# Gates of two branches as tile pairs with seven half-size products, in a phase of their own; branch sums kept in SBUF

## The chip, the core and the metric

The kernel runs on one core of one Trainium2 chip. A core has a matrix engine (PE), a vector engine (DVE), a scalar engine (ACT), a general engine (POOL) and an engine that mainly issues transfers (SP). Each runs its own list of instructions in order and waits for the others by semaphores. The time is device microseconds from start to end of one execution; a kernel's time is the median over its runs.

## What is computed

One decoder layer over 1024 tokens of width 1024, in float32:

```python
h    = rms_norm(x, g1)
proj = h @ w_in                        # heads of all branches, and 3 x 1024 gate logits
y_a  = rwkv7_branch(...)               # state recurrence over the tokens
y_b  = stick_breaking_branch(...)      # 8 heads of 64
y_m  = memory_branch(...)              # 4 heads of 128 on 256 memory tokens
branch_out = einsum('btnc,ncd->btnd', [y_a, y_b, y_m], w_branch)
merged = sum_b sigmoid(gate_logits_b) * branch_out_b
x = x + merged @ w_out
x = x + conv_ffn(rms_norm(x, g2), ...) # up-projection, causal convolution, SwiGLU, down-projection
```

The change touches the gate logits (`h @ w_in[:, gates]`), the sigmoid behind them, and the sum over the branches.

## The kernel before

The whole program is written out as one list per engine, with no loop left on the chip. Activations stand transposed in SBUF: 8 tiles of 128 channels x 1024 tokens, each split into a high part `xhi` and a low rest `xlo` that PE reads at its full speed. A weight tile of 128 output columns (`wr`, 128x1024) is split in the same way into `wh` and `wl`: ACT makes the high part (L83), POOL or DVE the rest (L89, L86). A float32 product is then three matmuls: hi by hi, lo by hi, hi by lo. The tokens' norm `rbc` is multiplied in behind the product.

A **gate** tile (`gate_item`, one branch b and one group d of 128 outputs) is such a projection: 8 channel tiles x 2 token halves x 3 = 48 matmuls of 128x512 into two PSUM banks "mm". ACT copies both banks to SBUF (L885), DVE multiplies with `rbc` (L886), ACT takes the sigmoid (L889), and for most gates the result goes to DRAM (`gsd`). There are 3 x 8 gates, 1152 such matmuls.

The order of the program is made by **weaving**: `weave(main, filler, ratio)` lets the main generator write one step and then as many steps of the filler as the ratio says. A filler step is one channel tile of a projection (6 matmuls) or of a branch (6 matmuls). The filler `pump` runs through a list `items`: projections of the rwkv branch, V, K and Q of stick-breaking, gates, the memory branch's projections, and the branch products (`branch_item`: y times `w_br`, 24 matmuls). The stages on the main side are `rwkv_prep` (four times), `sb_attn` (stick-breaking, L961), `mem_attn` (L1191), `stage2` (the state recurrence: 16 chunks of three steps, L601), `group_norm`. Behind them stand `branch_last`, `out_proj`, `up_phase` and `down_phase` with no weave.

Two places matter below. In `sb_qk` the K projection's two PSUM banks are copied by ACT and squared (`k_fin`), and then `k_ss` sums the squares over the heads with 32 small matmuls (`g<-kon,w` 64x2) on PE; in `items` a gate stands between the two (`kp, gate, kss`). And behind the memory branch `items` has three gates (`gate(sp1), gate(), gate()`) ahead of branch 1, whose input y was written to DRAM (`yd`) and is loaded again (`A<-yd`, `load_y`), split by ACT and DVE.

The sums over the branches go through a DRAM tensor `mrd`: branch 1 writes, branch 2 reads, adds and writes, `branch_last` reads.

PSUM has eight banks: four named "mm" for projections, four named "g" for everything else.

## Time and profile before

| | |
|---|---|
| time, median of 3 runs | 1786.67 us (1786.48 to 1787.19) |
| profiled execution: first to last instruction | 1785.0 us |
| PE busy | 1775.7 us, 99% |
| DVE / ACT / POOL busy | 1184.1 / 882.8 / 697.1 us |
| granted clock of PE, mean | 1.000 |
| `rwkv_prep` and before it | 0 to about 317 us |
| `sb_attn` | about 318 to 612 us |
| `mem_attn` | about 612 to 749 us |
| gates, first branch products | 749 to 785 us |
| `stage2` | about 785 to 983 us |
| the rest, to the end | 983 to 1785 us |

A row of the groups reads: line, engine, operation, output tile <- input tiles, shapes, count | busy us, mean ns of one | idle time of the engine just ahead of them and what ended it. The duration of a matmul in these rows is longer than its pitch, because matmuls overlap; its cost in a dense stretch is the stretch over the count. Line numbers with "of before" below are those of the kernel before; the changed kernel has other numbers.

### The profile page before, as it was taken

What the parts mean: (1) busy time and instruction counts of PE and PEld (TensorE: products, weight loads), DVE (VectorE), ACT (ScalarE), POOL (GpSimd) and SP (SyncE); (2) the same over time, 40 slices, a digit from 0 to 9 for tenths busy, and PEclk for the clock granted to TensorE, in tenths of its full rate; (3) what the DMA queues carried; (4) which work ended last, traced back from release to release, by engine and by line L of the source; (5) the groups of instructions that cost most, each with busy time, mean ns of one, the idle gap of its engine ahead of it and who ended that gap; (6) DMA issues with size and microseconds to landing.
All of it is one profiled execution on the core that took longest, in us unless ns stands there. A gap on an engine that the chain in (4) does not pass through costs nothing.

```text
span 1785.0 us, 27451 instructions
## 1 busy us (share of the span) xinstructions
PE 1775.7 (99%) x10481; PEld 1442.9 (81%) x10481; DVE 1184.1 (66%) x1687; ACT 882.8 (49%) x1667; POOL 697.1 (39%) x409
## 2 busy tenths in 40 slices
PE   9999999999999999999999999999999999999999
PEld 7777778878888888787777888888888888888887
DVE  5666674787888655243533882697767777795596
ACT  6543344466566635444556434454444445444343
POOL 1232252322221012022333322257777677545454
PEclk9999999999999999999999999999999999999999
DMA  4256574111112343658764662323323333396475
GB/s 185 72 167 188 180 247 152 51 56 43 54 57 69 111 126 93 201 181 280 264 229 146 236 210 98 115 89 124 101 89 110 109 109 113 109 330 219 142 248 200
DMA packets 120758, 263.39 MB, mean 148 GB/s; under 512 B 28330, under 2 KB 41130, under 8 KB 120499
## 3 DMA queue, kind: packets, MB, share of 16 engines
q1 hardware_dynamic: 82434, 193.31, 32.9%
q10 hardware_dynamic: 34416, 55.72, 8.5%
q0 software_dynamic: 3776, 12.62, 2.4%
q8 instruction: 82, 1.34, 0.3%
q14 instruction: 50, 0.40, 0.1%
HBM read 180.04 MB, written 81.53 MB: 147 GB/s over the span
## 4 chain that ended last, share of the span: by engine, by line
PE 62%; issue 1%; POOL 1%; ACT 1%; DVE 1%; DMA 0%; ACTq 0%; DVEq 0%; POOLq 0%; SPq 0%
PE mm L139 53%; PE g L139 8%; PE g L122 1%; POOL dw L1856 1%; DVE qk L715 0%; ACT wh L83 0%; DMA qk<-vd 0%; ACT w L885 0%; DVE w L886 0%; DVE keep L1876 0%; POOL l L1555 0%; ACT qk L664 0%; ACT ys L1020 0%; DVE wl L86 0%; ACT qk L1059 0%
## 5 line engine op out<-in xcount | busy, mean ns | idle before, releaser
L89 POOL TENSOR_TENSOR wl<-wr,wh 128x1024 fp32r<-128x1024 f32 x58 | 148.0, 2552 | 368.2 <-ACT wh L83 360.5
L139 PE MATMUL mm<-xhi,wh 128*128 128x512 f32 x784 | 260.6, 413 | 0.5 <-ACT w L936 0.4
L139 PE MATMUL mm<-xlo,wh 128*128 128x512 f32 x784 | 243.5, 392 | 0.7 <-DVE xlo L225 0.6
L139 PE MATMUL mm<-xhi,wl 128*128 128x512 f32 x784 | 242.2, 390 | 0.0
L139 PEld LDWEIGHTS mm<-xlo,wh 128*128 128x128 f32 x784 | 147.0, 188 | 34.0 <-DVE xlo L225 1.6
L139 PEld LDWEIGHTS mm<-xhi,wl 128*128 128x128 f32 x784 | 147.1, 188 | 32.6
L139 PEld LDWEIGHTS mm<-xhi,wh 128*128 128x128 f32 x784 | 136.5, 189 | 30.4 <-issue 7.9
L139 PE MATMUL mm<-dw,da 128*128 128x512 f32 x528 | 121.1, 390 | 0.0
L83 ACT ACTIVATE wh<-wr 128x1024 fp32r<-128x1024 f32 x75 | 79.5, 1060 | 81.0 <-PE mm L139 61.9
L139 PE MATMUL mm<-BT,l 128*128 128x512 f32 x504 | 118.0, 389 | 0.3 <-POOL l L1555 0.3
L139 PEld LDWEIGHTS mm<-dw,da 128*128 128x128 f32 x528 | 98.9, 188 | 21.7 <-DVE da L1855 1.2
L1856 POOL TENSOR_TENSOR dw<-draw,dw 128x512 fp32r<-128x512 f32 x55 | 83.1, 1520 | 77.0 <-ACT dw L1854 74.2
L985 DVE TENSOR_TENSOR_SCAN at<-at,at 128x128 f32<-128x128 f32 (+3 forms) x64 | 91.0, 1429 | 33.1 <-ACT at L979 33.0
L139 PEld LDWEIGHTS mm<-BT,l 128*128 128x128 f32 x504 | 94.5, 188 | 20.3 <-POOL l L1555 0.7
L139 PE MATMUL mm<-BT,wh 128*128 128x512 f32 x352 | 108.5, 389 | 0.1
L139 PE MATMUL mm<-B,wh 128*128 128x512 f32 x352 | 108.4, 389 | 0.0
L195 POOL TENSOR_TENSOR hf<-rs,half 128x16 f32<-128x16 f32 (+1 forms) x18 | 49.2, 2732 | 143.4 <-DVE rs L192 138.9
L1855 DVE TENSOR_TENSOR da<-draw,da 128x512 fp32r<-128x512 f32 x77 | 66.6, 873 | 49.0 <-ACT da L1853 48.6
L139 PE MATMUL g<-dw,da 128*128 128x512 f32 x396 | 90.5, 389 | 0.4 <-POOL dw L1856 0.4
L1853 ACT ACTIVATE da<-draw 128x512 fp32r<-128x512 f32 x77 | 48.3, 628 | 81.0 <-PE mm L139 31.7
L139 PEld LDWEIGHTS g<-dw,da 128*128 128x128 f32 x396 | 74.2, 188 | 16.2 <-POOL dw L1856 0.8
L1627 ACT ACTIVATE g<-u,params 128x512 f32<-128x512 f32 x88 | 65.2, 770 | 32.1 <-DVE u L1717 22.9
(345 smaller groups left out, 3956.6 us busy)
## 6 DMA issues: line engine op xcount, KB each, us to landing
wr<-in_w_in_dram SPq DMA_DIRECT2D x49, 512.0 KB, 3.8
draw<-actd SPq DMA_DIRECT2D x77, 256.0 KB, 3.1
at<-scr SPq DMA_DIRECT2D x28, 512.0 KB, 5.5
draw<-in_w_down_dram SPq DMA_DIRECT2D x55, 256.0 KB, 4.6
rw<-in_w_up_dram SPq DMA_DIRECT2D x22, 512.0 KB, 3.5
actd<-gall ACTq DMA_DIRECT2D x41, 256.0 KB, 3.1
gsd<-w ACTq DMA_DIRECT2D x20, 512.0 KB, 2.8
wr<-in_w_up_dram SPq DMA_DIRECT2D x18, 512.0 KB, 3.6
```

The source lines that it names most:

```text
L83: ins = self.nc.scalar.activation(hi, raw, AF.Copy)
L89: self.last_wl = self.nc.gpsimd.tensor_tensor(lo, raw, hi.bitcast(F32), ALU.subtract)
L122: self.pinned(self.nc.tensor.transpose(out, in_, self.ident[:n, :n]))
L139: self.pinned(self.nc.tensor.matmul(*a, **k))
L195: nc.gpsimd.tensor_tensor(out, t[:, :n], self.half[:, :n], ALU.pow)
L985: self.pinned(nc.vector.tensor_tensor_scan(sn[:, :W][:, ::-1], sn[:, :W][:, ::-1], self.smask[:, 1024 - W :][:, ::-1], 1.0, ALU.mult, ALU. ...
L1627: keep(nc.scalar.activation(c, u[:, 2 + h * 512 : 514 + h * 512], AF.Identity, scale=self.par("cw2", m), bias=self.par("cb", m)))
L1853: self.pinned(nc.scalar.activation(A[:, 0], a, AF.Copy))
L1855: self.pinned(nc.vector.tensor_tensor(A[:, 1], a, A[:, 0].bitcast(F32), ALU.subtract))
L1856: nc.gpsimd.tensor_tensor(Wt[:, 1], w, Wt[:, 0].bitcast(F32), ALU.subtract)
```

## The change

**Gate pairs.** The 16 gates of branches 1 and 2 are computed in pairs (d, d+1) with seven products of half size in place of eight: each is 4 channel tiles x 3 matmuls of 128x512, so 84 matmuls stand for 96. The left sides are `w1`, `w2` and sums of their halves, made per pair by POOL and split by ACT and POOL (`prep1` to `prep3`); the right sides are the halves of h and sums of these (`T12`, `T34`), made once by `x_sums` from the input that is loaded again. Products 1 and 2, 6 and 7, 5 and 3 share a PSUM bank; ACT and DVE add up the results, and all gates go to `gsd`.

**The phase.** `x_sums` is woven with V and three gates of branch 0 (`early`); `gate_pairs` follows, between `rwkv_prep` and `sb_attn`, with steps of the inversion (`inv`, DVE) beside it. The gates between K's projection and `kss` are gone, as are two of the three behind the memory branch. The weaves have new ratios: 0.55 for 1.03 (`sb_attn`), 1.4 for 1.6 (`mem_attn`), 1.1 for 2.08 (`stage2`).

**Sums in SBUF.** `mrd` is gone: the sums stay in tiles of `pool_l`, which is opened ahead of `stage2`, when h is no longer needed. The transfers of `inst<-mad` and `td<-inst` move from POOL's queue to SP's, and V is loaded again for its differences instead of being kept.

On PE the change takes 96 matmuls of 128x512 away and adds none.

```diff
@@ -896,7 +899,172 @@
...
+    def x_sums(self, gp):
+        nc = self.nc
+        self.T12, self.T34 = [], []
+        tags = iter(["qk"] * 8 + ["at"] * 7 + ["A"])
...
+        load(0)
+        for p in range(4):
+            nc.sync.dma_start(self.inst[p * 32 : p * 32 + 32], self.mad[p * 32 : p * 32 + 32])
+        yield
+        for k in range(4):
+            if k < 3:
+                load(k + 1)
+            x, z = raws.pop(k)
+            for t, i in ((x, k), (z, k + 4)):
+                self.pinned(nc.scalar.activation(t, t, AF.Copy, scale=self.par("g1", i)))
+            if k > 1:
+                next(gp)
+            yield
+            t12, t34 = self.t4(), self.t4()
+            sub(t12[:, L], x[:, R], x[:, L])
+            sub(t12[:, R], z[:, R], t12[:, L])
+            sub(t34[:, L], z[:, R], x[:, R])
+            sub(t34[:, R], t12[:, R], z[:, L])
+            yield
+            for t, out, eng in ((t12, self.T12, nc.vector), (t34, self.T34, nc.gpsimd)):
+                hi, lo = self.t4(next(tags), F32R), self.t4(next(tags), F32R)
+                self.pinned(nc.scalar.activation(hi, t, AF.Copy))
+                self.pinned(eng.tensor_tensor(lo, t, hi.bitcast(F32), ALU.subtract))
+                out.append((hi, lo))
+            yield
+        next(gp)
...
+    def gate_pairs(self, pairs, inv, steps, after):
...
+        X = (self.xhi, self.xlo)
+        plain = lambda k0, c: lambda v, k: X[v][k0 + k][:, c]
+        made = lambda T, c: lambda v, k: T[k][v][:, c]
+        side = {1: plain(0, L), 2: plain(4, L), 3: plain(4, R), 4: made(self.T34, R), 5: made(self.T12, L), 6: made(self.T12, R), 7: made(self.T34, L)}
+        pt = lambda o, x, y, op: nc.gpsimd.tensor_tensor(o, x, y, op)
+        vt = lambda o, x, y, op=ALU.add: self.pinned(nc.vector.tensor_tensor(o, x, y, op))
+
...
+        def prep1(n):
+            w = split(W[n][0], wt("wh"), wt("wl"))
+            st[n, 1], st[n, 2] = [[x[:, c] for x in w] for c in (L, R)]
+
+        def prep2(n):
+            w1, w2 = W[n]
+            s = st[n, "s"] = self.t4()
+            pt(s[:, L], w2[:, L], w2[:, R], ALU.add)
+            pt(s[:, R], s[:, L], w1[:, L], ALU.subtract)
+            w = split(s, self.t4("A", F32R), self.t4("A", F32R))
+            st[n, 5], st[n, 6] = [[x[:, c] for x in w] for c in (L, R)]
+
+        def prep3(n):
+            w1, w2 = W.pop(n)
+            s = st.pop((n, "s"))
+            pt(w2[:, L], w1[:, L], w2[:, L], ALU.subtract)
+            pt(w1[:, R], w1[:, R], s[:, R], ALU.subtract)
+            w = split(w2, wt("wh"), wt("wl"))
+            st[n, 7], st[n, 4] = [[x[:, c] for x in w] for c in (L, R)]
+            s4 = self.t4("A", F32R)
+            st[n, 3] = split(w1[:, R], s4[:, L], s4[:, R])
+
+        def product(n, i, bank, first):
+            w = st.pop((n, i))
+            for k in range(4):
+                for pi, (u, v) in enumerate(((0, 0), (0, 1), (1, 0))):
+                    self.mmul(bank, w[u][:, k * 128 : (k + 1) * 128], side[i](v, k), start=(first and k == 0 and pi == 0),
+                              stop=(k == 3 and pi == 2), skip_group_check=not first)
+
+        def finish(n, i, g):
+            b, d = pairs[n]
+            self.pinned(nc.scalar.activation(g, g, AF.Sigmoid))
+            nc.scalar.dma_start(self.gsd[b, d + i], g)
+
+        def step(n, i):
+            if i == 1:
+                A = st[n, "A"] = self.ps("mm")
+                product(n, 1, A, True)
+                st[n, "p1"] = self.t4("ys", n=512)
+                self.pinned(nc.scalar.activation(st[n, "p1"], A, AF.Copy))
...
+                B = st[n, "B"] = self.ps("mm")
+                product(n, 6, B, True)
+                u = st[n, "u"] = self.t4()
+                vt(u[:, R], B, st[n, "p1"])
...
+            elif i == 7:
+                B = st.pop((n, "B"))
+                product(n, 7, B, False)
+                v = st[n, "v"] = self.t4()
+                vt(v[:, L], B, st.pop((n, "p1")))
+                vt(v[:, R], st[n, "C"], v[:, L])
...
+            else:
+                C = st.pop((n, "C"))
+                product(n, 3, C, False)
+                u = st.pop((n, "u"))
+                vt(u[:, R], C, u[:, R])
+                vt(u[:, R], u[:, R], self.rbc[:, R], ALU.mult)
+                finish(n, 0, u)
...
+        for f in (load, prep1, prep2, prep3):
+            f(0)
+            if f != prep3:
+                yield
+        load(1)
+        due = 0.0
+        for n in range(len(pairs)):
+            for i in (1, 5, 6, 2, 7, 4, 3):
+                step(n, i)
+                if n + 1 == len(pairs):
+                    if i == 7:
+                        next(after)
+                else:
+                    if i == 2:
+                        prep1(n + 1)
+                    elif i == 7:
+                        prep2(n + 1)
+                    elif i == 3:
+                        prep3(n + 1)
+                        load(n + 2)
+                due += steps
+                while due >= 1.0:
+                    due -= 1.0
+                    next(inv, None)
+                yield
@@ -954,9 +1122,8 @@
 
         w = self.I["w_in"]
         hooks = {1: lambda: k_split(1), 3: q_ss, 4: lambda: q_split(0), 6: lambda: q_split(1)}
-        kq = {4: k_bc, 5: lambda: k_split(0)} if p else {5: k_bc, 6: lambda: k_split(0)}
-        kh = {} if p else {k: functools.partial(self.difference, k - 3) for k in (3, 4, 5, 6)}
-        return self.proj_item(w[18 + p], k_fin, kh), k_ss, self.proj_item(w[14 + p], q_fin, kq), hooks
+        kq = {4: k_bc, 5: lambda: k_split(0)} if p else {5: k_bc, 6: lambda: k_split(0)} | {k: functools.partial(self.difference, k - 1) for k in (1, 2, 3, 4)}
+        return self.proj_item(w[18 + p], k_fin, before), k_ss, self.proj_item(w[14 + p], q_fin, kq), hooks
@@ -1274,40 +1441,36 @@
...
+            yield
+        if first:
+            self.merged.append(self.part("o") if d < 5 else g)
+        out = self.merged[d] if first else g
         for h in range(2):
             hs = slice(h * 512, (h + 1) * 512)
-            self.pinned(nc.vector.tensor_tensor(g[:, hs], pp[h], g[:, hs], ALU.mult))
+            self.pinned(nc.vector.tensor_tensor(out[:, hs], pp[h], g[:, hs], ALU.mult))
         if not first:
-            (nc.vector if d == 7 else nc.gpsimd).tensor_tensor(g, g, o, ALU.add)
-        nc.gpsimd.dma_start(self.mrd[d], g)
@@ -1970,49 +2138,49 @@
...
-        gq = [(b, d) for b in (1, 0) for d in range(8)]
-        gq[14:14] = [(2, d) for d in range(4)]
-        self.stored = set(gq)
...
+        gq = [(0, d) for d in range(8)]
...
+        items = [self.shift_item(i + p, krv[p], f"{n}{p}") for p in range(4) for n, i in (("k", 4), ("r", 0), ("v", 8)) if (p, n) != (0, "k")]
+        items += [*self.sb_v(), gate(), gate(), gate()]
+        early = self.stream(items)
+        items = []
+        hooks = {0: self.differ}
         for p in range(4):
-            kp, kss, qp, hooks = self.sb_qk(p, qk[p])
-            items += [*([self.differ] if p == 0 else []), kp, gate({4: self.spread_last} if p == 0 else {}), kss, qp, gate(hooks), mark(f"sb{p}")]
+            kp, kss, qp, after = self.sb_qk(p, qk[p], hooks)
+            items += [kp, *([mark(f"sb{p - 1}")] if p else []), kss, qp]
+            hooks = after | ({5: self.spread_last} if p == 0 else {})
         prep, mss, mv, mk = self.mem_kv()
...
-            mqi[h] = self.mem_q(h, mq[h], {2: mqi[h - 1][1], 4: mark(f"mq{h - 1}")} if h > 1 else {})
-        items += [gate({0: prep[0], 5: prep[1]}), gate(), lambda: setattr(self, "low_dve", True), gate({2: prep[0], 6: prep[1]}), mss, *mv, *mk, mqi[0][0], mark("kv")]
-        items += [self.mem_kss, gate({3: mqi[0][1]}), self.mem_kbc, mqi[1][0], mark("mq0")]
-        items += [mqi[2][0], mqi[3][0], gate({2: mqi[3][1], 4: mark("mq3")}), gate(), mark("mem")]
-        ld1, br1, sp1 = self.branch(1, True)
+            mqi[h] = self.mem_q(h, mq[h], {2: mqi[h - 1][1], 4: mark(f"mq{h - 1}")} if h > 1 else {3: mqi[0][1]} if h else {})
+        items += [gate(hooks), mark("sb3"), gate({0: prep[0], 5: prep[1]}), lambda: setattr(self, "low_dve", True), gate({2: prep[0], 6: prep[1]})]
+        items += [mss, *mv, *mk, mqi[0][0], mark("kv"), self.mem_kss, mqi[1][0], self.mem_kbc, mark("mq0"), mqi[2][0], mqi[3][0]]
+        items += [gate({2: mqi[3][1], 4: mark("mq3")}), mark("mem")]
         ld2, br2, sp2 = self.branch(2, False)
-        items += [lambda: drain(inv), ld1, gate(sp1), gate(), gate(), mark("y1"), *br1, ld2, gate(sp2), *br2, gate(), gate()]
+        ld1, br1, sp1 = self.branch(1, True, {(1, 3): ld2} | {(k + 1, 1): f for k, f in sp2.items()})
+        items += [lambda: drain(inv), ld1, gate(sp1), mark("y1"), *br1, *br2]
@@ -2023,34 +2191,40 @@
...
...
+        gp = self.gate_pairs([(b, d) for b in (1, 2) for d in (0, 2, 4, 6)], inv, 1.15, pump)
+        self.weave(self.x_sums(gp), early, 1.9, 0)
+        drain(early)
+        early = None
+        self.close_gates()
+        drain(gp)
         pace[0] = 6
         self.guard = True
         need("sb0")
-        self.weave(self.sb_attn(qk, need), pump, 1.03, 0)
+        self.weave(self.sb_attn(qk, need), pump, 0.55, 0)
         pace[0] = 11
         need("kv")
         self.late = True
-        self.weave(self.mem_attn(mq, need), pump, 1.6, 0)
+        self.weave(self.mem_attn(mq, need), pump, 1.4, 0)
         need("mem")
...
+        self.close_gates()
+        sx.close()
+        self.pool_l = sl.enter_context(tc.tile_pool(name="l4", bufs=16))
         self.strict = True
-        self.weave(st2, pump, 2.08, 0)
+        self.weave(st2, pump, 1.1, 0)
         self.weave(self.group_norm(), pump, 1.0, 0)
         self.strict = False
         drain(pump)
-        self.close_gates()
         self.pin = False
-        sx.close()
-        self.pool_l = sl.enter_context(tc.tile_pool(name="l4", bufs=16))
         self.branch_last()
```

How the order of instructions stands at two places. The first is the end of the last of the three gates and the start of the first pair. On PE the 12 matmuls of the pair's product 1 follow the gate's last matmul directly, and behind them stands product 5, whose first row waits for ACT (the high part `A_418` of its left side) and whose third waits for POOL (the rest `A_419`). On DVE, in the changed kernel, `w4_410` is that last gate, which ACT copies out of PSUM ahead of this, and `w4_411` and `w4_412` are the sums of the fourth round of `x_sums`:

```order
L937 TENSOR_TENSOR at_405_2481<-w4_402_2460,at_404_2480 128x1024 [waits DMAHW7_49,DMAHW3_49,Activation_49]
L889 TENSOR_TENSOR w4_410_2512<-w4_410_2512,rbc_343 128x1024 [waits DMAHW3_49,Activation_49]
L907 TENSOR_TENSOR w4_411_2516<-A_398_2438 128x512 [waits DVE_49]
L907 TENSOR_TENSOR w4_411_2516<-A_399_2439,w4_411_2516 128x512 [waits DVE_49]
L907 TENSOR_TENSOR w4_412_2517<-A_399_2439,A_398_2438 128x512 [waits Pool_49]
L907 TENSOR_TENSOR w4_412_2517<-w4_411_2516,A_399_2439 128x512 [waits DVE_49]
L937 TENSOR_TENSOR at_414_2523<-w4_411_2516,at_413_2522 128x1024 [waits DMAHW5_49,DMAHW4_49,Activation_49]
```

The multiplication of the gate stands ahead of the four subtractions of the fourth round. On POOL there stand the low rests of `T34` (L937), the sums of the weight halves (L950, 128x512) and their splits:

```order
L937 TENSOR_TENSOR at_407_2485<-w4_403_2461,at_406_2484 128x1024 [waits DMAHW6_49,DMAHW3_49,Activation_49]
L937 TENSOR_TENSOR A_416_2527<-w4_412_2517,at_415_2526 128x1024 [waits Activation_49]
L950 TENSOR_TENSOR w4_417_2530<-wr_401_2445 128x512 [waits DMAHW2_49,DVE_49]
L950 TENSOR_TENSOR w4_417_2530<-w4_417_2530,X_400_2444 128x512 [waits Pool_49]
L950 TENSOR_TENSOR wr_401_2445<-X_400_2444,wr_401_2445 128x512
L950 TENSOR_TENSOR X_400_2444<-X_400_2444,w4_417_2530 128x512 [waits Pool_49]
L950 TENSOR_TENSOR A_419_2534<-w4_417_2530,A_418_2533 128x1024 [waits Activation_49]
L950 TENSOR_TENSOR wl_421_2542<-wr_401_2445,wh_420_2541 128x1024 [waits PE_49,Activation_49]
```

The sum for product 5, `w4_417`, stands behind the last low rest of `T34` (`A_416`), which reads what DVE's last subtraction wrote; the rest `A_419` that product 5 reads stands behind two more sums.

The second place is K's projection and the sum of its squares. PE before, at the first of the four: the end of K (`mm_372`, `mm_373`), a gate (`mm_384`, `mm_385`), the small matmuls `g_391`, and Q.

```order
L139 MATMUL mm_372_2269<-xhi7_121,wl_353_2179 128x512
L139 MATMUL mm_373_2270<-xhi7_121,wl_353_2179 128x512
L139 MATMUL mm_384_2354<-xhi0_114,wh_370_2265 128x512 [waits Activation_49]
L139 MATMUL mm_385_2355<-xhi0_114,wh_370_2265 128x512
...
L139 MATMUL mm_384_2354<-xhi7_121,wl_371_2266 128x512
L139 MATMUL mm_385_2355<-xhi7_121,wl_371_2266 128x512
L139 MATMUL g_391_2433<-kon_69,w4_379_2342 64x2 [waits Activation_49]
L139 MATMUL mm_399_2466<-xhi0_114,wh_382_2350 128x512
L139 MATMUL mm_400_2467<-xhi0_114,wh_382_2350 128x512
```

PE in the changed kernel at the same K (`mm_587`, `mm_588`), with `w4_602` the squares:

```order
L139 MATMUL mm_587_3656<-xlo7_128,wh_579_3607 128x512
L139 MATMUL mm_588_3657<-xlo7_128,wh_579_3607 128x512
L139 MATMUL mm_587_3656<-xhi7_120,wl_580_3608 128x512
L139 MATMUL mm_588_3657<-xhi7_120,wl_580_3608 128x512
L139 MATMUL g_603_3738<-kon_69,w4_602_3734 64x2 [waits PE_49,Activation_49]
L139 MATMUL mm_612_3772<-xhi0_113,wh_585_3652 128x512 [waits DVE_49]
L139 MATMUL mm_613_3773<-xhi0_113,wh_585_3652 128x512 [waits DVE_49]
```

The gate's 48 matmuls no longer stand between the two. On ACT the changed kernel has four rows from K's end to the squares: the two copies out of PSUM, the split of a weight tile (L83 of before), and the squares.

122 lines of the change are left out of this document (78 added, 44 removed).

## The prediction

> **What bounds the kernel now.** I read the page first, for the engines and the slices, then PE's waits, then single stretches.
>
> ```profile
> span 1785.0 us, 27451 instructions
> PE 1775.7 (99%) x10481; PEld 1442.9 (81%) x10481; DVE 1184.1 (66%) x1687; ACT 882.8 (49%) x1667; POOL 697.1 (39%) x409
> PE   9999999999999999999999999999999999999999
> PEclk9999999999999999999999999999999999999999
> ```
>
> PE is busy in every slice and at full clock; no other engine comes near. The waits of PE by releaser:
>
> ```profile
> engine line waited for: us in total, times, longest us
> PE g L139 <- DVE qk L202: 1.5, 1, 1.5
> PE g L122 <- ACT at L997: 0.6, 1, 0.6
> PE mm L139 <- DVE xlo L225: 0.6, 1, 0.6
> ```
>
> Nine rows in all, 5 us together, the longest 1.5 us. So PE's list runs through without a hole, and the kernel's time is the sum of PE's matmuls. A matmul taken away is then worth its pitch, and every wait that the change puts in costs its full length. The pitch is read from a stretch with gates alone, and beside it stands the start of the program:
>
> ```profile
> core 0: us, PE busy (x), PEclk, DMA share, GB/s
> 1.50:6.50 5.00, 5.00 (x12) 1.00 0.93 337
> 754.50:776.50 22.00, 22.00 (x98) 1.00 0.50 182
> ```
>
> Of 98 records two are cut by the edges, so 97 lie in it: 22.00 / 97 = 0.2268 us. A longer stretch of gates, quoted at the end, gives 26.00 / 116 = 0.2241. I take 0.2265; the choice moves the sum by 0.2 us. In the first 5 us of the run a matmul takes 5.00 / 12 = 0.417 or, by the same reasoning, a little more.
>
> **1. Matmuls taken away: -21.7.** 96 x 0.2265 = 21.7. Nothing is added on PE, so this is the whole gain. The sums kept in SBUF, the missing writes and reads of `mrd`, and the transfers moved to SP's queue give PE nothing: none of its waits names a transfer. They cost nothing either as long as they stay hidden: `td` now stands among SP's weight loads, 16 short issues over the whole phase, where PE uses one weight tile per 48 matmuls, 10.9 us; without that cover a load would come late by a landing.
>
> ```profile
> wr<-in_w_in_dram SPq DMA_DIRECT2D x49, 512.0 KB, 3.8
> td<-inst POOLq DMA_DIRECT2D x16, 128.0 KB, 5.2
> ```
>
> **2. The first pair's product 5: +13.2.** The order shows what is queued. When the last gate's final matmul ends, PE has product 1 left (12 x 0.2265 = 2.7 us) and two rows of product 5 (0.45). Everything else must still be made, in a chain over three engines, each in order:
>
> ```profile
> L885 ACT ACTIVATE w<-mm 128x512 f32<-128x512 f32 x48 | 26.0, 594 | 33.2 <-PE mm L139 32.5 <-issue 0.6
> L889 ACT ACTIVATE w<-w 128x1024 f32<-128x1024 f32 x24 | 25.4, 1057 | 17.0 <-DVE w L886 16.9
> L83 ACT ACTIVATE wh<-wr 128x1024 fp32r<-128x1024 f32 x75 | 79.5, 1060 | 81.0 <-PE mm L139 61.9 <-issue 13.7 <-DMA scr<-qk 2.2
> L86 DVE TENSOR_TENSOR wl<-wr,wh 128x1024 fp32r<-128x1024 f32 x17 | 20.7, 1219 | 8.7 <-ACT wh L83 8.4
> L886 DVE TENSOR_TENSOR w<-w,rbc 128x1024 f32<-128x1024 f32 x24 | 44.4, 1848 | 54.8 <-ACT w L885 54.7
> L1297 DVE TENSOR_TENSOR w<-mm,w 128x512 f32<-128x512 f32 x32 | 20.6, 684 | 17.8 <-PE mm L139 13.6 <-DMA w<-gsd 4.2
> L1555 POOL TENSOR_TENSOR l<-it,l 128x1024 fp32r<-128x1024 f32 x20 | 48.0, 2400 | 84.5 <-ACT l L1554 84.5
> L1582 POOL TENSOR_TENSOR wr<-wr,wr 128x512 f32<-128x512 f32 x10 | 12.9, 1291 | 0.0
> ```
>
> ACT copies the gate's two banks: 1.1 (two of 0.59). DVE multiplies the gate: 1.22 to 1.85, because this stands ahead of the fourth round's subtractions. Four subtractions of 0.68: 2.7. ACT makes the high part of `T34`: 1.06. POOL makes its rest: 2.4. Only now come the two sums for product 5, 2 x 1.29 = 2.6, and ACT's high part, 1.06. That is 12.1 to 12.8 us after the gate's end, and the first row of product 5 is free. Its third row needs POOL's rest, behind two more sums: from the sums' end at 11.1 to 11.7, 2 x 1.29 + 2.4 = 5.0, so 16.1 to 16.7. PE had 3.2 us of work: idle for 12.9 to 13.5 us. I take 13.2; bounds 10 (every piece at its shortest, the gate's multiplication hidden) and 15 (a hop of a tenth of a us between engines, and L886 at its mean).
>
> **3. A cold start behind it: +2.** No wait of this kernel is longer than 1.5 us, so no row shows PE after a long pause, except the start: there twelve matmuls took 0.417 in place of 0.2265, 2.3 us more. If a pause of 13 us makes PE start again in the same way, it costs that; if the start's pitch came from something else, nothing. The clock row gives 1.00 there, which speaks against; I take 2 of the 0 to 2.3, since nothing else in those rows explains a pitch near twice the usual. The Trainium skill ("TensorE: Matmul & The Clock Gate", Part 1) says that PE's clock falls to half after an idle window of about 3.4 us and comes back after about as long under load. By it the loss would be an estimated 1.7 us here, and as much at any other pause above 3.4 us; no run here shows it yet.
>
> **4. The other seven pairs: +2.5.** A pair is 84 matmuls, 19.0 us. From the end of product 2 to that of product 3, and on to the next pair's product 5, PE has 48 matmuls and two, 11.3 us. In this time ACT and POOL make the next pair's sums: 1.06 + 2.4 + four sums of 1.29 to 1.55 + 2.4, thus 11.0 to 12.1 us. A loss of 0 to 0.8 per pair; 0 to 6 in all.
>
> **5. K's squares: +6.4.** With no gate between K and the sum of its squares, PE waits for what stands on ACT. Before, the gate's copies were the last thing on ACT, and the small matmuls followed the gate at once:
>
> ```profile
> 289.16 0.61 PE L139 MATMUL mm<-xhi,wl 128*128 128x512 f32 x2
> 289.59 1.08 ACT L885 ACTIVATE w<-mm 128x512 f32<-128x512 f32 x2 [9.18 <-PE mm L139]
> 289.71 1.10 PE L139 MATMUL g<-kon,w 128*64 128x2 f32 x32
> ```
>
> Now two copies (1.08), a split of a weight (1.06) and the squares (1.06) lie between K's end and the sum: 3.2 us for the first head pair and, with the same rows queued, for the second. Bounds 2 x 2.1 (the split done earlier) and 2 x 3.5. The third and fourth come while stick-breaking runs and are counted there.
>
> **6. Stick-breaking: +6.** Its main steps are mixed with filler, which the change halves.
>
> ```profile
> core 0: us, PE busy (x) PEld busy (x) DVE busy (x) ACT busy (x) POOL busy (x), PEclk, DMA share, GB/s
> 317.70:612.20 294.50, 293.45 (x2036) 239.33 (x2036) 236.33 (x207) 178.63 (x338) 64.82 (x27) 1.00 0.18 59
> ...
> 784.80:983.00 198.20, 197.46 (x2076) 155.18 (x2076) 78.86 (x236) 106.98 (x399) 64.17 (x38) 1.00 0.67 229
> ```
>
> By the order 336 projection matmuls (76.1 us) and about 12 us of the memory's keys and values leave the stage, which leaves 206 us of PE. ACT has 178.6 us now; nine gates or so go with their copies, sigmoids (L889) and splits (9 x 3.3), some 150 are left, and with DVE's steps between them ACT is loaded three quarters where it was three fifths.
>
> ```profile
> L979 ACT ACTIVATE at<-g,nf 128x512 f32<-128x512 f32 x48 | 32.2, 688 | 23.8 <-PE g L139 19.1 <-ACT ys L1020 4.0 <-DVE at L985 0.6
> L1020 ACT ACTIVATE ys<-mm,jk 64x128 f32<-64x128 f32 x64 | 19.8, 357 | 47.1 <-PE mm L139 46.9
> ```
>
> ACT waits for PE in these rows now: about 66 us over the 64 blocks, 1.0 us a block. The filler that leaves is 76.1 / 64 = 1.2 us a block, so the reserve is used up, on average, and blocks below the average make PE wait. Bounds: 0, and 18 (a quarter of what left, where each block is short of 0.28). I take 6, of which some 2.5 for the third K, whose squares stand behind stick-breaking's own work on ACT.
>
> **7. Memory to branch 1: +2.5.** The last quarter of y can be loaded when the memory branch lets go of its buffer:
>
> ```profile
> 748.01 1.45 PE L139 MATMUL mm<-at,A 128*128 128x512 f32 x3
> 749.49 0.32 SPq L1261 DMA_DIRECT2D A<-yd  x1
> A<-yd SPq DMA_DIRECT2D x8, 512.0 KB, 6.2
> ```
>
> Then 6.2 us of landing, 1.06 and 1.22 of splitting: 8.5 us. Before, 132 gate matmuls (30 us) covered this; now 18 matmuls of the quarters ahead, 4.1 us. At 6.2 us of landing PE waits 4.4; if the loads land sooner or the other quarters are late by less, nothing.
>
> **8. The recurrence: +4.** Of the 198.2 us, by the order, about 132 us of 512-column filler fall to about 66; a chunk is then 8.2 us of PE for 12.4. ACT has 107.0 / 16 = 6.7 us a chunk, and the steps hang on each other:
>
> ```profile
> L676 ACT ACTIVATE qk<-g 64x64 f32<-64x64 f32 x128 | 28.0, 219 | 28.1 <-DVE ys L674 26.0
> L664 ACT ACTIVATE qk<-g 64x64 f32<-64x64 f32 x128 | 28.0, 219 | 28.8 <-PE g L139 26.4 <-ACT w L889 0.4
> ```
>
> ACT's own waits of 57 us for 16 chunks, 3.6 a chunk, are about the 4.2 us that go. 0 to 9, that is up to 0.19 for each of 48 steps; I take 4.
>
> **Sum.** -21.7 + 13.2 + 2 + 2.5 + 6.4 + 6 + 2.5 + 4 = +14.9. The profiled execution has 1785.0 us, so 1799.9, and the median of the runs lies 1.7 above the span: 1801.6.
>
> **Rivals.**
>
> *Faster.* The hidden terms 3, 4, 6, 7, 8 are nothing and the first pair's chain is shorter than its rows, since only the gate's multiplication and one round would have to run sooner: -21.7 + 10 + 4.2 = -7.5, about 1779. For it: PE waited 5 us in all in the kernel before, with ACT and DVE as often between its rows. Against: there the cover was twice as long. It holds if the wait ahead of product 5 is 10 us or less and stick-breaking and the recurrence lose under 2 each.
>
> *No change.* Only the firm waits, 13.2 + 6.4 = 19.6, against 21.7: -2.1, about 1784.6, with a us or two of the soft terms 1786. Its condition is that ACT's reserve in stick-breaking and the recurrence lasts.
>
> *Much slower: ACT sets the pace.* In stick-breaking the three engines follow each other within a block, and four "g" banks couple them. If the cover no longer suffices, PE waits in most blocks: 18 there, 9 in the recurrence, 6 over the pairs, and with the firm 19.6, 2.3 and 4.4 about +38, 1824. It decides from 0.28 us a block on. For it: ACT's reserve of 1.0 a block against 1.2 taken. Against: ACT's list also gets shorter by the gates.
>
> **Chances.** Forecast (between 1790 and 1815) 0.54; much slower 0.16; no change 0.14; faster 0.16. A measurement of this kernel tells about 0.2% (3.6 us) from no change, so: faster 0.16, same 0.14, slower 0.70. The range leaves out a tenth on each side: from between the faster and the equal case, 1780, to 1822, ahead of the worst.
>
> **What would show it.** PE's waits should have one of about 13 us, released by POOL, at the first pair; two of 3 us at the small matmuls `g<-kon,w` released by ACT; a pitch above 0.4 for some 12 matmuls behind the long wait, and in stick-breaking and the recurrence many waits below 1 us. The gates' stretch must still run at the present pitch:
>
> ```profile
> 751.00:777.00 26.00, 26.00 (x117) 21.51 (x115) 6.18 (x3) 8.21 (x10) 4.79 (x2) 1.00 0.55 199
> ```
>
> Wrong would be the forecast if the wait at product 5 is under 8 us, if ACT stays below two thirds in stick-breaking with PE dense, or if a wait appears that names a transfer of SP's queue.

## The result: 6.8% slower, 1908.74 us

The changed kernel takes 1908.74 us (median of 4 runs, 1908.15 to 1911.07) against 1786.93 us of the kernel before on the same chip: ratio 1.0683, 95% interval 1.0668 to 1.0698. The forecast was 1801.6 us with a range up to 1822. The sign was right and the size was not: +122 us in place of +15. The page of the changed kernel, its first lines and two of its slices:

```profile
span 1909.1 us, 27379 instructions
PE 1806.0 (95%) x10385; PEld 1457.0 (76%) x10385; DVE 1268.1 (66%) x1753; ACT 899.2 (47%) x1675; POOL 776.7 (41%) x427
PE   9999997988989899889899879999999999999999
PEclk9999998999899999989999989999999999999999
```

There are 96 matmuls fewer (10481 - 10385), as planned. PE is busy for 95% of a longer span, and it is busy *longer* than before, 1806.0 us for 1775.7, with less to do. Two things must have happened: PE waits, and its matmuls got slower. The waits:

```profile
engine line waited for: us in total, times, longest us
PE mm L139 <- POOL A L950: 19.9, 8, 3.8
PE mm L139 <- ACT A L964: 10.6, 1, 10.6
PE mm L139 <- ACT at L1164: 9.0, 5, 3.4
PE mm L139 <- ACT wh L83: 7.6, 4, 2.3
PE g L139 <- DVE ys L654: 5.9, 2, 4.5
PE mm L139 <- ACT qk L732: 5.5, 1, 5.5
PE g L139 <- ACT at L1146: 5.1, 3, 1.8
PE g L139 <- ACT w L1076: 5.1, 2, 2.8
PE mm L139 <- ACT w L888: 4.8, 1, 4.8
...
```

Where there were nine rows with 5 us of waits together, there are now some 95 us, at every stage from the pairs to the group norm. Their places, in windows over the changed kernel (the columns are those of the windows in the prediction; PEclk is the mean granted clock): the pairs; the first K and Q; stick-breaking; the memory branch; branch 1's start and the recurrence; the group norm; the rest.

```profile
300.00:507.00 207.00, 176.12 (x719) 141.35 (x718) 165.93 (x138) 57.12 (x66) 143.13 (x68) 0.92 0.29 105
507.00:530.00 23.00, 20.54 (x109) 17.18 (x110) 15.12 (x17) 6.82 (x10) 5.55 (x4) 0.85 0.08 24
530.00:784.00 254.00, 229.03 (x1716) 184.26 (x1715) 175.46 (x171) 158.69 (x315) 47.06 (x22) 0.96 0.12 36
784.00:940.00 156.00, 141.32 (x892) 115.48 (x891) 56.77 (x119) 70.58 (x147) 10.27 (x11) 0.95 0.40 124
940.00:1096.00 156.00, 142.74 (x1730) 107.14 (x1729) 67.94 (x224) 90.39 (x364) 34.76 (x14) 0.97 0.64 219
1096.00:1134.00 38.00, 29.63 (x193) 22.66 (x191) 27.44 (x51) 12.30 (x42) 15.89 (x7) 0.86 0.29 98
1134.00:1909.10 775.10, 768.79 (x3400) 633.34 (x3400) 563.74 (x805) 353.85 (x560) 425.84 (x260) 1.00 0.43 146
```

The last row is as long as before (775 us to the same point of the program there: 773.5). Nearly all of the loss lies between 300 and 1134 us, and in each of these windows the clock is below 1.00. What such a clock does to a matmul shows in two neighbouring windows, both without a gap:

```profile
core 0: us, PE busy (x), PEclk, DMA share, GB/s
1136.00:1140.70 4.70, 4.70 (x10) 0.50 0.91 329
1141.00:1145.70 4.70, 4.70 (x22) 1.00 0.93 340
```

At 0.50 ten matmuls fall into 4.7 us, at 1.00 twenty-two. By the starts in the trace the pitch is 0.43 us in the first window, once the rows are of one kind, and 0.23 in the second: it doubles, nearly. The trace's clock record has 17 stretches at 0.50 in this kernel up to its last matmul, 105.8 us together, each 3.41 us or a multiple of it; that of the kernel before has none.

With this the 124.1 us between the two profiled executions come apart. PE without any matmul in flight, between its first and its last: 98.0 us for 4.0. Matmuls in flight at half clock: 84.9 us, of which half, 42.5, would not have been needed. This is an account and not yet an experiment: it takes it that nothing else would have held PE up meanwhile.

| profiled execution, against the kernel before | span | matmuls added or removed x 0.2265 | idle PE | half clock | rest |
|---|---|---|---|---|---|
| the change | +124.1 | -21.7 | +94.0 | +42.5 | +9.3 |

The rest, 4 to 11 us in all the kernels below, lies in time that counts as busy. Waits shorter than a matmul is long would hide there, since their ends are modelled; that is argued, not shown.

### The profile page after: what moved, and what is told of

The parts are those of the page before. It is cut to its first block, busy times and chain, and to the rows that moved or that the text cites. A ratio compares the mean times of both kernels' runs of the same rounds, so it can differ in the third digit from the quotient of the medians.

```text
span 1909.1 us, 27379 instructions
## 1 busy us (share of the span) xinstructions
PE 1806.0 (95%) x10385; PEld 1457.0 (76%) x10385; DVE 1268.1 (66%) x1753; ACT 899.2 (47%) x1675; POOL 776.7 (41%) x427
## 4 chain that ended last, share of the span: by engine, by line
PE 55%; ACT 3%; issue 3%; DVE 3%; POOL 2%; DMA 0%; ACTq 0%; DVEq 0%; POOLq 0%
PE mm L139 46%; PE g L139 7%; PE g L122 2%; POOL dw L2024 1%; DVE qk L713 1%; ACT qk L674 0%; ACT jk L704 0%; ACT qk L662 0%; ACT wh L83 0%; DVE wl L86 0%; ACT at L1146 0%; DVE A L733 0%; POOL hf L194 0%; POOL wl L89 0%; ACT ys L1187 0%
## 5 line engine op out<-in xcount | busy, mean ns | idle before, releaser
L89 POOL TENSOR_TENSOR wl<-wr,wh 128x1024 fp32r<-128x1024 f32 x44 | 110.7, 2517 | 394.2 <-ACT wh L83 366.8
L139 PE MATMUL mm<-xhi,wh 128*128 128x512 f32 x592 | 203.2, 416 | 0.1
L139 PE MATMUL mm<-xlo,wh 128*128 128x512 f32 x592 | 191.0, 395 | 0.6 <-DVE xlo L224 0.6
L139 PE MATMUL mm<-xhi,wl 128*128 128x512 f32 x592 | 190.1, 394 | 0.0
L139 PEld LDWEIGHTS mm<-xlo,wh 128*128 128x128 f32 x592 | 112.4, 190 | 26.1 <-DVE xlo L224 1.4
L139 PEld LDWEIGHTS mm<-xhi,wl 128*128 128x128 f32 x592 | 112.6, 190 | 24.8
L139 PEld LDWEIGHTS mm<-xhi,wh 128*128 128x128 f32 x592 | 105.5, 191 | 24.3 <-issue 7.5
L139 PEld LDWEIGHTS mm<-dw,da 128*128 128x128 f32 x528 | 99.0, 188 | 21.3 <-DVE da L2023 0.8
L139 PE MATMUL mm<-at,A 128*64 128x128 f32 (+1 forms) x704 | 92.0, 325 | 9.1 <-ACT at L1164 9.0
L83 ACT ACTIVATE wh<-wr 128x1024 fp32r<-128x1024 f32 x59 | 62.5, 1061 | 70.5 <-PE mm L139 50.4
L139 PEld LDWEIGHTS mm<-at,A 128*64 128x64 f32 (+1 forms) x704 | 65.4, 156 | 30.0 <-issue 12.2
```

The lines of the kernel that those rows point to most:

```text
L83: ins = self.nc.scalar.activation(hi, raw, AF.Copy)
L89: self.last_wl = self.nc.gpsimd.tensor_tensor(lo, raw, hi.bitcast(F32), ALU.subtract)
L139: self.pinned(self.nc.tensor.matmul(*a, **k))
```

## Experiments

The theory from this trace had three parts: (1) the new *place* costs more than the seven products, because the gates that are computed ahead are missing as filler in stick-breaking, the memory branch, the recurrence and the group norm; (2) in the phase of the pairs POOL is too slow, and it is DVE's inversion beside it that slows it; (3) the clock adds about half as much again to what the waits cost. The rival to (1) is that the pairs' sums are the cause; to (2), that POOL's own chain is too long; to (3), that only waits count.

### The clock: filling the waits with useless matmuls

```diff
             elif i == 5:
                 C = st[n, "C"] = self.ps("mm")
+                for _ in range((54, 3, 5, 9, 12, 14, 16, 17)[n]):
+                    self.mmul(C, st[n, 2][0][:, 0:128], X[0][4][:, L], start=True, stop=True)
                 product(n, 5, C, True)
```

> The changed kernel with 130 extra matmuls of 128x512 (54 ahead of the first pair's product 5, then 3, 5, 9, 12, 14, 16, 17 ahead of the other pairs' product 5), into the bank that product 5 then starts afresh. They take up the time in which PE waited there in the changed kernel (13.1 us at the first pair, 0.6 to 3.8 us at the others, 30.5 us in all; 130 x 0.2265 = 29.4 us). Theory: a wait costs its own length and, if it takes most of a window of 3.4 us, half of the following window or windows, because the granted clock falls to 0.5. Then the extra work is nearly free and the stretch of the pairs, 313 to 501 us, gets shorter by what the clock took there, 4.3 + 8.8 = 13 us: about 1896, granted clock near 1.00 in the stretch. Rival: only the waits count and the clock in the records slows nothing: 1907 to 1912.

Measured: 1903.89 us (1899.98 to 1906.49), ratio 1.0658 (1.0640 to 1.0676); the profiled execution 1898.1 us for 1909.1. The window of the pairs, as the first one above:

```profile
300.00:498.00 198.00, 194.18 (x845) 157.47 (x844) 167.00 (x138) 55.25 (x63) 143.79 (x68) 1.00 0.31 110
```

198 us for 207, at clock 1.00 for 0.92, with 126 more matmul records in it. PE idles 3.8 us in place of 30.9: some 27 us of waiting were exchanged for 29.4 us of useless work, and the stretch got *shorter*. The two windows do not begin and end at quite the same matmuls; from the first matmul of the pairs to the last ahead of the first K's squares it is 207.0 us in the changed kernel (299.6 to 506.6) and 199.5 here (298.7 to 498.2). So about 10 us of it had been the clock. Of the 84.9 us at half clock 22 lie in this stretch, and half of that, by the account above, is 11.

The medians tell less: they differ by only 5 us, the four runs spread over 6.5 us, the profiled one is the fastest of them, and the intervals of the two ratios just overlap. All four lie below the 1907 to 1912 of the rival, and all four above the 1896 of the theory. What speaks against the rival is the stretch.

### The first pair's chain

```diff
-        self.weave(self.x_sums(gp), early, 1.9, 0)
+        self.weave(self.x_sums(gp), early, 1.2, 0)
```

> The changed kernel with the weave of x_sums against the early projections at 1.2 in place of 1.9, so that the fourth round of sums and the first pair's sums are written ahead of the last gate's end. Theory (the first pair's chain behind the last gate's end is the cause of the 13.1 us wait): the wait falls to 3 us or less, and with it go the 17 us at half clock around it, 8 us: about 1890. Rival (the chain is bound by the loads of x or by POOL all through the rounds): the wait moves into the rounds or stays, 1903 to 1910.

Measured: 1913.26 us (1909.12 to 1913.85), ratio 1.0701 (1.0685 to 1.0717): no gain, and above what either side expected. The two waits at product 5 went from 10.6 and 2.5 us to 7.6 and 2.5. The fourth round now stands behind the multiplication of the gate before the last. In this run's timeline ACT copies that gate at 295.4 us, late, behind its work for the earlier rounds; DVE multiplies at 296.5 and ends the round's subtractions at 301.0, and product 5 gets its first operand at 309.2, 7.6 us after PE ran out of work. So the rival is nearer: the wait stays, in the main, because the rounds as a whole are late under V and three gates.

### No inversion beside the pairs

```diff
-        gp = self.gate_pairs([...], inv, 1.15, pump)
+        gp = self.gate_pairs([...], inv, 0.0, pump)
```

> The changed kernel with no step of the inversion beside the pairs; the steps run later, beside stick-breaking and the memory branch. Theory A (DVE's steps of the inversion slow POOL's instructions, whose 128x512 sums grow from 1.27 to 2.27 us over the pairs): POOL's sums stay at 1.3 us, the waits at product 5 of pairs 2 to 8, 17.4 us together, fall under 4, and the stretch's clock rises from 0.95 to 0.98 or more: 13 us of waits and 6 us of clock less there. Rival B (POOL's and ACT's chain of a pair is too long by itself): the waits stay above 10 us. The total may lie anywhere from 1885 to 1912, since the steps come back in later stages; the verdict is read in the stretch of the pairs.

Measured: 1896.72 us (1889.58 to 1899.32), ratio 1.0607 (1.0585 to 1.0629). The waits at product 5 of pairs 2 to 8, which grew in the changed kernel as 0.6, 1.1, 2.1, 2.8, 3.3, 3.6 and 3.8 us, are now 0.98 us each, seven times: 6.9 us in place of 17.4, more than the 4 that the theory allowed and less than the rival's 10. The clock from 325 us to the end of the pairs is 1.00 for 0.95. POOL's groups in the pairs, first of the changed kernel and then without the inversion:

```profile
L950 POOL TENSOR_TENSOR X<-X,w 128x512 f32<-128x512 f32 x7 | 14.8, 2119 | 0.0
L950 POOL TENSOR_TENSOR wr<-X,wr 128x512 f32<-128x512 f32 x7 | 13.9, 1985 | 0.0
...
L950 POOL TENSOR_TENSOR w<-w,X 128x512 f32<-128x512 f32 x7 | 12.4, 1776 | 0.6
```

```profile
L950 POOL TENSOR_TENSOR X<-X,w 128x512 f32<-128x512 f32 x8 | 17.3, 2162 | 0.0
...
L950 POOL TENSOR_TENSOR wr<-X,wr 128x512 f32<-128x512 f32 x7 | 9.1, 1302 | 0.0
...
L950 POOL TENSOR_TENSOR w<-w,X 128x512 f32<-128x512 f32 x7 | 9.0, 1288 | 0.5
```

The two lower sums take 1.29 and 1.30 us alone and 1.78 and 1.99 beside the inversion, whose instructions get longer from pair to pair. The upper one, `X<-X,w`, takes some 2.1 us in both kernels: without the inversion it is DVE's multiplication of the pair's own gate with `rbc` that stands beside it (2.10 us at 434 us of that run; the same shape takes 1.23 elsewhere). How, the changed kernel's timeline shows late in the phase:

```profile
445.34 2.20 DVE L588 TENSOR_TENSOR inst<-inst,it 128x920 f32<-128x920 f32 x1
446.52 2.16 POOL L950 TENSOR_TENSOR X<-X,w 128x512 f32<-128x512 f32 x1
447.57 2.10 DVE L586 TENSOR_TENSOR it<-inst 128x936 f32<-128x936 f32 x1
448.65 3.23 POOL L950 TENSOR_TENSOR A<-w,A 128x1024 fp32r<-128x1024 f32 x1
...
457.83 1.15 DVE L588 TENSOR_TENSOR inst<-inst,it 128x950 f32<-128x950 f32 x1
```

An inversion step takes 1.15 us alone and about 2.1 next to POOL, POOL's sum 2.16 for 1.29: each ends 0.9 to 1 us late, as if they took turns. The Trainium skill ("SBUF — State Buffer", section "SBUF: two separate sides") says so: DVE and GpSimd share one pair of ports as an exclusive lock for the whole instruction, where DVE has two inputs in SBUF and GpSimd reads there. These rows agree, 1.15 to 2.1 and 1.29 to 2.16 us. Theory (2) is shown for the growth from pair to pair. The 0.98 us that are left are about what the upper sum still loses beside DVE (2.16 - 1.29); no run took that away.

The stretch of the pairs got 18 us shorter, near the 19 expected of it (188.8 us for 207.0). The median fell by 12, because the inversion now piles up in the memory branch (a wait of 7.8 us there is new, and one of 4.8 grew to 6.9).

### The same place with plain gates

```diff
-        items += [*self.sb_v(), gate(), gate(), gate()]
+        items += [*self.sb_v(), gate(), gate(), gate(), *[self.gate_item(b, d) for b in (1, 2) for d in range(8)]]
...
-        gp = self.gate_pairs(...)
-        self.weave(self.x_sums(gp), early, 1.9, 0)
...
```

With the pairs go `x_sums` and the weave of both; the inversion runs beside the 16 plain gates, half a step for each filler step.

> The changed kernel's order, stages and sums in SBUF, but the 16 gates of branches 1 and 2 computed in the same phase as plain gates of 48 matmuls, without x_sums and pairs (96 matmuls more on PE). Theory (the new place costs more than the seven products): the phase runs without waits and at clock 1.00: 1908.7 - 30.5 of waits - 13 of clock + 21.7 = about 1887; the stages behind it keep their lengths. Rival (nearly all of the loss comes from the pairs' sums): 1787 to 1815.

Measured: 1877.00 us (1874.24 to 1877.10), ratio 1.0499 (1.0483 to 1.0515). With 96 matmuls *more* this is 32 us faster than the change. The phase has no wait above 0.3 us up to the first K. The rival (the pairs alone, under 1815) falls, and theory (1) carries most: +90 us come from the new order without a single pair. That the run lies 10 us below the 1887 expected goes with the memory branch's keys and values, which wait 10.5 us in the change and 0.8 here.

### Filler alone, in the kernel before

If (1) is right, nearly halving stick-breaking's filler must cost in the kernel before as well, which has no pairs and all its gates where they were.

```diff
-        self.weave(self.sb_attn(qk, need), pump, 1.03, 0)
+        self.weave(self.sb_attn(qk, need), pump, 0.55, 0)
```

The other run has 0.8 at the same place.

> The kernel before with one number changed: the weave of stick-breaking takes 0.55 filler steps per main step, as the changed kernel does, in place of 1.03. No matmul is added or taken away; the filler that stick-breaking no longer takes up (its projections and gates) runs behind it, densely. Theory (the waits of the changed kernel in stick-breaking, 22 us in 540 to 794, come from the halved filler): waits of 15 to 25 us and 5 to 12 us of half clock appear in a kernel that has no pairs and all its gates: 1807 to 1824. Rival (they come from where the changed kernel puts K, Q and the gates, not from the share of filler): 1787 to 1793.

> The same with 0.8: a quarter of the filler less in place of nearly half. Theory (a reserve of ACT that is used up step by step; the waits set in where the filler of a step falls under the other engines' chain): if the loss grows with what is missing, half of that of the 0.55 run; if there is a reserve, under 3 us: between 1787 and 1800, and the two runs together tell which. Rival as above: 1787.

Measured: at 0.55, 1825.49 us (1822.52 to 1828.35), ratio 1.0215 (1.0197 to 1.0233); at 0.80, 1813.74 us (1811.87 to 1815.83), ratio 1.0151 (1.0135 to 1.0167). The waits at 0.55:

```profile
PE g L139 <- ACT at L979: 4.8, 3, 2.4
PE mm L139 <- ACT w L936: 4.7, 3, 2.5
PE mm L139 <- DVE wl L86: 4.1, 6, 1.5
PE mm L139 <- ACT at L997: 3.3, 3, 1.8
```

One number, not one matmul more, and 38 us are lost. Of PE's waits some 21 us lie in stick-breaking, inside the 15 to 25 expected; the third row stands behind it, at the memory branch's keys and values. A quarter of the filler less costs 27 us already, so there is no reserve, and the loss is not in proportion either: the first quarter costs more than the second. Both times lie above the range expected, 1825 for 1824 at most and 1814 for 1800. The rival, that the share of filler costs nothing, is out.

### Smaller numbers of the change

```diff
-        self.weave(st2, pump, 1.1, 0)
+        self.weave(st2, pump, 0.9, 0)
```

> The changed kernel with one number changed: the recurrence takes 0.9 filler steps per main step in place of 1.1, so that some ten steps of the branch products are left for the group norm behind it. Theory (the 10 us of waits and the 17 us at half clock at 1117 to 1152 come from the filler having run out ahead of the group norm): waits there fall under 4 us and the half clock under 7 us, while the recurrence waits 0 to 4 us more: 10 us less, about 1898. Rival (the waits there come from the group norm's own chain, whatever filler there is): 1905 to 1913.

Measured: 1907.20 us (1903.28 to 1910.61), ratio 1.0679 (1.0661 to 1.0697): not to be told from the change, and in the rival's range (1905 to 1913). In its trace the waits near the group norm are still there, one of 5.3 us ahead of branch 2's product and one of 2.1: the wait changed its place. The half clock around them fell from 17 to 7 us and the profiled execution is 7.6 us shorter, but the runs do not bear that out.

> The changed kernel with four of its numbers changed together: no inversion beside the pairs, the inversion's pace beside stick-breaking 13 in place of 6 (so that it does not pile up in the memory branch), x_sums at 1.2, the recurrence at 0.9. Theory (these are the parts of the loss that do not hang on the missing gates): waits of the pairs 17 -> 7, first pair 13 -> 10, group norm 10 -> 4, with their half clock: 1870 to 1885, still far above the kernel before, since the waits in stick-breaking (22 us) and at the memory branch (15 us) stay. Rival (the rest hangs on these numbers too): under 1850.

Its edit is the two one-line changes above (0.0 beside the pairs, 1.2 for x_sums), 0.9 for the recurrence, and `pace[0] = 13` for 6. Measured: 1901.76 us (1901.15 to 1903.11), ratio 1.0643 (1.0628 to 1.0659), outside what either side expected. The pairs' waits are 0.97 us each as foreseen, but with pace 13 the inversion meets stick-breaking: a wait of 7.5 us appears at its start, with 17 us at half clock around it. These numbers only push the loss about.

### The filler given back

The strongest test of (1): all else of the change (sums in SBUF, transfers on SP's queue, V loaded again, the recurrence without gates), but plain gates, 15 of them again in stick-breaking and the memory branch as in the kernel before, and 9 ahead.

```diff
+        items += [*self.sb_v(), *[gate() for _ in range(9)]]
...
+            items += [kp, gate({5: self.spread_last} if p == 0 else {}), kss, qp, gate(after), mark(f"sb{p}")]
...
+        self.weave(self.sb_attn(qk, need), pump, 1.03, 0)
...
+        self.weave(self.mem_attn(mq, need), pump, 1.6, 0)
```

> The sums in SBUF and the moved transfers of the changed kernel, no pairs, all 24 gates plain; 9 gates run ahead of stick-breaking, and 15 stand again where the kernel before has them in stick-breaking and the memory branch, with its shares of filler, 1.03 and 1.6. Only the recurrence and the group norm stay without gates (1.1). Theory (the loss of the new place is the missing filler, stage by stage): no wait above 1 us ahead of the memory branch's end; left are about 5 us at branch 1's y, 8 in the recurrence, 10 at the group norm, some 12 for half clock there and 5 that no wait shows: 1822 to 1830. Rival (the sums in SBUF, V loaded again or the moved transfers cost time themselves): waits in stick-breaking, above 1840.

Measured: 1821.81 us (1820.81 to 1823.25), ratio 1.0186 (1.0168 to 1.0204), 55 us below the plain gates of the phase with the same matmuls.

```profile
PE g L139 <- DMA qk<-vd: 3.6, 1, 3.6
PE g L139 <- ACT w L1105: 3.3, 1, 3.3
PE mm L139 <- ACT qk L732: 3.1, 1, 3.1
PE g L139 <- DVE ys L654: 3.0, 1, 3.0
...
```

Stick-breaking and the memory branch have no wait above 0.7 us any more; one of 3.3 us at the first Q's squares (L1105) is left ahead of them. The 34 us that remain lie, but for that wait and its half clock, behind: at the start of the recurrence (waits of 1.6 and 3.6 us for two loads that land late), in it, and at the group norm. So the loss of the place splits into about 55 us for stick-breaking and the memory branch and 34 for the rest. The rival (above 1840) is out. No run gave the gates back to the recurrence and the group norm, so that missing filler is the cause of the 34 us as well is argued, not shown. No wait points at the sums in SBUF; whether the transfers that moved to SP's queue have a part in the two late loads, which are issued there, is open.

### The same with three pairs

Six of the nine gates ahead as three pairs, 36 matmuls fewer, without the inversion beside them, and the first pair's sums hooked into the last plain gate:

```diff
+        items += [*self.sb_v(), gate(), gate(), gate({0: go, 4: go})]
...
+        gp = self.gate_pairs([(1, 0), (1, 2), (1, 4)], inv, 0.0, pump)
+        self.weave(self.x_sums(gp), early, 1.2, 0)
```

(`go` writes the next of the first pair's preparations.)

> The same, with six of the nine gates ahead of stick-breaking as three pairs (36 matmuls fewer, 8.2 us), no inversion beside them, and the first pair's sums written under the last of three plain gates. Theory (where the sums are made in time and the filler is left alone, the seven products earn what they save): 8.2 less, 2 to 3 us of waits at the second and third pair, 0 to 4 at the first: 2 to 6 us less than the run without pairs. Rival (x_sums cannot be covered by V and three gates): a wait of 7 us or more at the first pair with its half clock, 3 us less to 10 us more than the run without pairs.

Measured: 1825.09 us (1824.80 to 1829.38), ratio 1.0214 (1.0196 to 1.0232), 3 us above the run without pairs: the theory (2 to 6 less) fails, and the time lies in the rival's range (3 less to 10 more).

```profile
PE mm L139 <- POOL A L949: 5.3, 3, 3.4
PE mm L139 <- ACT qk L732: 4.7, 1, 4.7
PE mm L139 <- ACT yhi L1433: 4.3, 1, 4.3
```

The first pair still waits about 6 us in four pieces, the others 0.97 each; together that is the 8.2 us saved. Elsewhere waits changed both ways: the two late loads, 5.2 us, are gone, but branch 1's y, which waited 1 us, now waits 4.3, and the wait at L732 grew from 3.1 to 4.7. Why, no run tells; the inversion, which ran beside the plain gates there, runs later here. Even where the filler is kept, the seven products at best break even here.

All profiled executions in the same account, against the 1785.0 us of the kernel before:

| kernel | span | matmuls x 0.2265 | idle PE | half clock | rest |
|---|---|---|---|---|---|
| the change | +124.1 | -21.7 | +94.0 | +42.5 | +9.3 |
| waits filled | +113.1 | -21.7 + 29.4 | +65.7 | +29.6 | +10.1 |
| x_sums at 1.2 | +122.3 | -21.7 | +92.4 | +41.8 | +9.8 |
| no inversion beside the pairs | +102.8 | -21.7 | +87.3 | +26.8 | +10.4 |
| plain gates in the phase | +87.5 | 0 | +56.4 | +24.6 | +6.5 |
| before, stick-breaking at 0.55 | +39.1 | 0 | +26.6 | +6.8 | +5.7 |
| before, stick-breaking at 0.80 | +25.1 | 0 | +15.4 | +5.1 | +4.6 |
| the recurrence at 0.9 | +116.5 | -21.7 | +92.8 | +37.1 | +8.3 |
| four numbers together | +114.3 | -21.7 | +92.5 | +32.5 | +11.0 |
| filler given back | +36.5 | 0 | +21.3 | +11.4 | +3.8 |
| filler given back, three pairs | +37.9 | -8.2 | +29.5 | +11.0 | +5.6 |

No version tried beats the kernel before. Pairs as filler inside stick-breaking were not tried: their sums of h need sixteen tiles that K, Q and the attention use there.

## Why the prediction was wrong

**What bounds the kernel, and term 1: right.** PE's list was full, and each wait cost its length at least. The 96 matmuls went.

**Term 2, the first pair (13.2 us): right in length and mechanism.** Measured 10.6 + 2.5 = 13.1 us, by the chain that was written down; the larger part is released by ACT's high part and not by POOL, as the prediction's first sign had it. The changed kernel's timeline, from the gate's copies to product 5's third row:

```profile
301.06 1.06 ACT L888 ACTIVATE w<-mm 128x512 f32<-128x512 f32 x2
302.15 1.23 DVE L889 TENSOR_TENSOR w<-w,rbc 128x1024 f32<-128x1024 f32 x1 [3.02 <-ACT w L888]
...
305.22 0.68 DVE L907 TENSOR_TENSOR w<-w,A 128x512 f32<-128x512 f32 x1
...
307.07 2.34 POOL L937 TENSOR_TENSOR A<-w,at 128x1024 fp32r<-128x1024 f32 x1 [5.52 <-ACT at L936]
...
310.71 1.26 POOL L950 TENSOR_TENSOR w<-w,X 128x512 f32<-128x512 f32 x1
...
313.11 1.22 PE L139 MATMUL mm<-qk,A 128*128 128x512 f32 x2 [10.63 <-ACT A L964]
...
314.40 2.34 POOL L950 TENSOR_TENSOR A<-w,A 128x1024 fp32r<-128x1024 f32 x1
...
316.79 2.08 PE L139 MATMUL mm<-qk,A 128*128 128x512 f32 x4 [2.45 <-POOL A L950]
```

What was not seen is that taking one link away (the gate's multiplication) would have helped by 3 us only, as the run with x_sums at 1.2 shows: the rounds of x_sums are late as a whole.

**Term 3, the cold start (+2): the largest failure of one term, 42.5 us.** The mechanism was named, but charged once, at the one long pause. "The clock row gives 1.00 there, which speaks against" was a misreading: the clock record of the kernel before begins only at 6.7 us. Up to there its matmuls start 0.43 us apart, and from 11 us on 0.23; the pitch was the true witness. And the rule was taken to need a pause of 3.4 us. The clock record of the changed kernel shows otherwise: the clock is set anew every 3.41 us, and a wait of 2.8 us (the first K's squares) was followed by 6.8 us at half clock. In the eleven kernels here that have half clock, 108 of the 115 windows of 3.41 us at full clock that were followed by half clock had PE idle for more than half of the window (the other seven for 0.23 to 0.44), and no window followed by full clock had it idle for more than 0.58. The windows after which the clock came back had PE idle for 0.21 at most: where the last 0.6 us of a wait reached into the next window (the seventh pair), the clock stayed at half for another. Eleven windows with 0.07 or less stayed at half all the same, so this is not the whole rule. The Trainium skill ("TensorE: Matmul & The Clock Gate", Part 1) has the two states and the windows of 3.41 us right, as this trace shows; its "idle window" is here a window idle for about half. By the rule as the prediction took it, 1.7 us for each of the seven waits above 3.4 us, the loss would have been 12 us.

**Term 4, the other pairs (+2.5, at most 6): 17.4 us.** POOL's sums were priced at 1.29 to 1.55 us from rows of other stages. The change itself puts the inversion beside them, which the prediction had read in the order and not priced. Without it the chain costs 0.98 a pair, near the upper bound that was worked out, 0.8; that part is POOL beside DVE's multiplication and not the longer of two prices for a sum.

**Term 5, K's squares (+6.4): right.** 2.8 + 2.3 = 5.1 us.

**Term 6, stick-breaking (+6, at most 18): 22 us of waits.** The step that failed is the reserve: ACT's waits of "1.0 us a block", set against the filler that leaves, "so the reserve is used up, on average". An engine's idle time is not a reserve for PE: within a block PE, ACT and DVE follow each other, and what covers PE is filler at the very place where its next operand is late. The run at 0.80 shows it: 27 us lost, though ACT is busy for only 57% of the stage (161.2 of 282.3 us). In the changed kernel ACT's busy share, which was to tell, is 158.69 / 254 = 62%, about what it was (61%), and not the three quarters forecast. An ACT share below two thirds was to be a sign against the forecast if PE was dense there. PE is not: it is busy for 90%, with thirteen waits of 0.4 to 3.4 us, together above the 18 that were to be the worst case. The wait for the third K's squares, 2.5 of the 6, does not show.

**Term 7, branch 1's y (+2.5, at most 4.4): 4.8 us, right in the main.** The last quarter of y is late, as foreseen. But what PE waits for in the end is a bank: on ACT the gate's copy out of PSUM stands behind the split of that quarter.

```profile
945.29 1.06 ACT L1434 ACTIVATE yhi<-A 128x1024 fp32r<-128x1024 f32 x1 [4.49 <-DMA A<-yd]
946.25 1.07 ACT L888 ACTIVATE w<-mm 128x512 f32<-128x512 f32 x2
...
946.89 0.80 PE L139 MATMUL mm<-yhi,wh 128*128 128x512 f32 x1 [4.78 <-ACT w L888]
```

**Term 8, the recurrence (+4): 5.9 us, near in size, and not by the steps that hang on each other.** Many waits below 1 us were forecast. There are two, of 1.4 and 4.5 us, and both end with a copy on DVE that stands behind the statistics of the group norm there:

```profile
1084.66 3.66 DVE L713 TENSOR_SCALAR qk<-qk,hn,hf 128x64 f32<-128x64 f32 x16 [3.60 <-POOL hf L194]
...
1089.48 1.06 PE L139 MATMUL g<-ys,qk 64*64 64x64 f32 x16 [4.54 <-DVE ys L654]
```

At the same copy (L656 of before) the kernel before has one wait, of 0.5 us. That the size came out is in part luck.

**Not foreseen at all: 25 us.** The memory branch's keys and values (10.5 us of waits, released by ACT's and DVE's splits: the split of the next weight stands behind the copies of the last result) and its first scores (4.1, behind the split of the finished keys); and the group norm (10 us), which two gates had covered and which has no filler left. The waits of the keys and values hang on the order on ACT: in the run without the inversion beside the pairs and in that with plain gates in the phase these splits run about one weight ahead of PE, and 2.2 and 0.8 us are left. The prediction looked for cover at the places where gates had been taken away next to a row it knew, and not at every stage that the filler list used to feed.

In sum: the measured waits are 13.1 + 17.4 + 5.1 + 22 + 14.7 + 4.8 + 5.9 + 10.1 = 93 us against 35 foreseen, and the clock 42.5 against 2. The likeliest rival on that side, "ACT sets the pace", named the place and not the cause: ACT was no busier than before.

## What to carry to other kernels

Work that hides waits is worth more than its own time: ahead of moving it out of a stage, cut that stage's filler by one number in the kernel as it is and time that (here 38 us for nearly half, against 21.7 to be won in all). Count a wait of PE of some 2 us or more with the half clock that follows it, here 0.45 us for each us of waiting, over all waits (42.5 / 94.0). Work moved to POOL is to be priced beside what DVE does in that stage, not by its duration when alone.
